# A hybrid attention and RWKV-7 trunk step: prices of the builder's clock, and attention steps ordered a quarter microsecond behind it

## The chip, the cores and the metric

One NeuronCore of one Trainium2 chip. The metric is the device time of one execution in microseconds; of several executions the median counts.

## The reference

One layer of a streaming encoder runs on 512 prompt tokens and on 8 streams of 16 new tokens, 640 tokens in all, with a model width of 1024:

```python
h = rmsnorm(x, norm_g)
proj = h @ w_in                      # [q k v z_a | g_a g_b | r k v lat_w lat_a z_b]
# A: stick-breaking attention, 16 heads of 64, weight
#    sigmoid(z[t,s]) * prod_{s<j<t} (1 - sigmoid(z[t,j])), s < t
y_a = (o_a * silu(z_a)) @ w_o_a
# B: RWKV-7 with a token shift, state S per head
S = S * w_t + (S @ -kk_t) (kk_t * a_t) + v_t k_t ;  o_t = S r_t
y_b = (norm(o_b) * silu(z_b)) @ w_o_b
x = x + (sigmoid(g_a) * y_a + sigmoid(g_b) * y_b) @ w_out
y = rmsnorm(x, final_norm_g)
```

All is in float32. The streams bring 128 past keys and values per head and a state of 64 x 64 per head. The outputs are `y`, the new keys and values, the last projected row and the new states.

## The kernel before, in words

**Work.** The tokens lie along the columns, 640 of them. A projection is a *job*: 128 columns of a weight matrix, split into a high and a low part (`whi`, `wlo`) by ScalarE and VectorE, against `xh` and `xl`, the split input, in two halves of some 320 tokens. Each half is 8 steps of three matmuls (`gemm_range`, L500), so a job has 48 matmuls into the PSUM tiles `ps_g`. There are 73 jobs of the input projection that feed both mixers, then 8 for the gate of B (`cons_gb`), 8 with `w_o_b`, 8 with `w_o_a`, and last `w_out`. The last gate job frees `xh` and `xl` part by part (`xfree`); the stream `reload` (L1542) then fills them with mixer B's output `oB` and, when attention has ended, fills `oAh` and `oAl` with mixer A's output. The jobs with `w_o_b` wait for those parts, those with `w_o_a` for `oAh`.

**RWKV stage.** For each of 8 pairs of heads there are streams `prep`, `prep2`, `samp` and `chain`. `samp` reads the sample states, four transfers into `s0r` (`state_load`, L718: 64 partitions, three dimensions), and transposes them. Its small products use 16, 32 or 64 rows of the array.

**Attention stage.** When RWKV's last pair is done, `open_attn` (L1569) spawns for each pair of heads `aprep` (loads, transposes of keys and values) and `attn` (L1294). `attn` goes through nine items: one for the samples and eight blocks of prompt queries (4, 4, 3, 3, 2, 2, 1, 1 key blocks). For each there is a `score` (two matmuls into `ps_a`; two sigmoids on ScalarE to `kp` and `bt`; a mask on `bt` by POOL; a running product of `kp` and a product into `bt` on VectorE), two items later a `flip` (transposes of `bt` into `ps_b`, copied to `wt`), and then `pv` (products with the values into `ps_c`). In `pv` of the sample item there are 16 products with the past values `Vp`, of 16 columns each, and 4 of 64 columns.

**What sets the order.** The program is written out once, at build time, in one order per engine, and each engine goes through its instructions in that order. The order comes from a clock that the builder keeps: every instruction that is issued goes through `_Eng` (L206), which gives it a duration by operation and shape, and `Clock.note` (L136) moves the engine's time on and notes when each tile will be ready. `Driver.run` (L304) looks at TensorE's time `now` and takes the stream of the highest rank whose awaited tiles are ready by then (`at <= now + 0.02`). If there is none, the main program goes on, and that is the next step of a projection. Only when the main program has to wait as well is the stream taken that will be ready first. Ranks: `chain` 0, `reload` 1, `prep2`, `samp` and `attn` 2, `prep` and `aprep` 3; a lower number goes first. All transfers are issued by SP.

The lines of the choice, with `s[2]` the awaited tiles:

```python
at = self.clk.at(s[2])
if at <= now + 0.02 and (best is None or s[:2] < best[:2]):
    best = s
if soon is None or at < soon[0]:
    soon = (at, s)
```

In the profile every instruction that goes through the builder's wrapper has line L214, so groups are told apart by tiles. A product of two float32 tiles stands in it as two matmuls, one of float32r tiles as one.

Of the kernel before, what the change touches and what calls it, by code (L numbers as in the profile page):

```python
# [162 lines left out]
def _name(ap):  # L163

    if not hasattr(ap, "tensor"):
        return ap
    n = ap.tensor.name
    return f"{n}:{ap.offset % (8 * T) // T}" if n in PARTS else n


def _cols(ap):
    n = 1
    for d in ap.shape[1:]:
        n *= d
    return n
# [30 lines left out]
class _Eng:  # L206
# [3 lines left out]
    def __getattr__(self, op):  # L210
        f = getattr(self.obj, op)

        def call(*a, **k):
            r = f(*a, **k)  # L214
            aps = [x for x in list(a) + list(k.values()) if hasattr(x, "tensor")]
            out = k.get("out", aps[0])
            ins = [x for k, x in enumerate(aps) if x is not out or any(x is y for y in aps[:k])]
            n = _cols(out)
            e = self.eng
            lat = Clock.LAT  # L220
            if e == "pe":
                w = k.get("lhsT")
                m, r = (128, 128) if w is None else (_cols(w), w.shape[0])
                if w is None:
                    d = 0.109
                elif w.dtype == F32R:
                    d = max(0.013 + n / 2400.0, 0.107)
                elif w.dtype == F32:
                    d = max(0.026 + n * 0.00087, 0.082 if m > 32 else 0.041) if m <= 64 else \
                        max(n / 600.0 + 0.005, 0.216)  # L230
                else:
                    d = 0.089
                mode = "full" if r > 64 and m > 64 else (r > 32, r > 64, m > 32, m > 64)
                if mode != self.clk.mode:
                    d += 0.1 if self.clk.mode == "full" else 0.2
                    self.clk.mode = mode
            elif e == "act":
                d = 0.065 + n * 0.00085 + 0.1 * sum(hasattr(k.get(x), "tensor") for x in ("scale", "bias"))
                if out.shape[0] < 64:
                    d = 0.12 + n * 0.0021  # L240
                elif out.shape[0] < 128:
                    d += 0.115
                fn = str(k.get("func"))
                t = "sig" if "Sigmoid" in fn or "Tanh" in fn else "exp" if "Exp" in fn else \
                    "sqrt" if "Sqrt" in fn else None
                if t is not None and t != self.clk.tbl:
                    self.clk.tbl = t
                    d += 1.28
            elif e == "dve":
                d = 0.075 + n * 0.00106  # L250
                if op == "scalar_tensor_tensor":
                    d = 0.13 + n * 0.00112
                elif op == "tensor_scalar":
                    d = 0.1 + n * 0.0011 + 0.03 * sum(hasattr(x, "tensor") and _cols(x) == 1
                                                     for x in list(a) + list(k.values()))
                elif op == "tensor_tensor_scan":
                    d = 0.03 + n * 0.0025
                elif op == "reciprocal":
                    d = 0.05 + n * 0.0064
                elif op == "bn_stats":  # L260
                    d = 0.126
                elif op == "transpose" and len(ins[0].shape) > 2 and ins[0].ap[-1][0] > 1:
                    d = 2.03
                if out.shape[0] < 128 and any(_name(x).startswith("ps_") for x in ins if hasattr(x, "tensor")):
                    d += 0.09
            elif e == "pool":
                d = 0.2 + n * (0.0022 if op == "tensor_tensor" else 0.0012)
                if op == "tensor_copy":
                    d = 0.15 + n * 0.0035
            else:  # L270
                d = 0.47
                run = 2.0 if min(x.shape[-1] for x in aps) < 128 else 1.0
                lat = (n * out.shape[0] * 4 * run / 3.6e5, 0.65, 0.93)
            self.clk.note(e, d, [_name(x) for x in ins], [_name(out)], lat)
            return r
        return call


class Driver:
# [6 lines left out]
        self.streams = []  # L286
        self.n = 0

    def spawn(self, gen, prio):
        self.n += 1  # L290
        self.streams.append([prio, self.n, [], None, gen])

    def _step(self, s):
        try:
# [9 lines left out]
    def run(self, main):  # L304
        gate, done, need = None, False, []
        while not done or self.streams:
            now = self.clk.free["pe"]
            self.each(now)
            best, soon = None, None
            for s in self.streams:  # L310
                if s[3] is not None:
                    if not s[3]():
                        continue
                    s[3], s[2] = None, []
                at = self.clk.at(s[2])
                if at <= now + 0.02 and (best is None or s[:2] < best[:2]):
                    best = s
                if soon is None or at < soon[0]:
                    soon = (at, s)
            if best is not None:  # L320
                self._step(best)
                continue
            if not done and (gate is None or gate()):
                gate = None
                at = self.clk.at(need)
                if at <= now + 0.02 or soon is None or at <= soon[0]:
                    need = []
                    try:
                        y = next(main)
                    except StopIteration:  # L330
                        done = True
                        continue
                    if callable(y):
                        gate = y
                    elif y is not None:
                        need = list(y)
                    continue
            assert soon is not None, "streams wait on each other"
            self._step(soon[1])


def body(tc, ins, outs, dbg=None):
# [4 lines left out]
    drv = Driver(clk)  # L347
    es = ExitStack()

    def pool(name, bufs=1, side="left", **kw):  # L350
        return _Pool(clk, tc.tile_pool(name=name, bufs=bufs, side=side, reuse_waits="tile", **kw),
                     name, bufs)
# [828 lines left out]
    at, ap = {}, {}  # L1181
# [240 lines left out]
    with tc.manual_schedule():  # L1422
# [146 lines left out]
        def open_attn():  # L1569
            if ap:  # L1570
                return
            es3.close()
            es1.close()
            tr_cm.__exit__(None, None, None)
            h["m"] = es.enter_context(pool("m")).tile([128, 8, T], F32, name="m")
            ap["rl"] = es.enter_context(pool("rl"))
            ap["ap2"] = es2.enter_context(pool("ap2", bufs=2))
            ap["ap1"] = es2.enter_context(pool("ap1", bufs=1))
            ap["as2"] = es2.enter_context(pool("as2", bufs=3))
            ap["msk"] = ap["ap1"].tile([128, 640], F32, name="amsk")  # L1580
            dma(out=ap["msk"], in_=ins["consts"][:, NC:NC + 640])
            bft = ap["as2"].tile([128, 256], F32, tag="kp", name="bft", bufs=2)
            dma(out=bft, in_=ins["consts"][:, NC + 640:NC + 896])
            ap["bf"] = ap["ap1"].tile([128, 3, 128], BF16, name="bfc")
            V.tensor_copy(ap["bf"][:, 0, :], ident)
            V.tensor_copy(ap["bf"][:, 1:3].rearrange("p q x -> p (q x)"), bft)
            for p in range(NPAIR):
                drv.spawn(aprep(p), 3)
                drv.spawn(attn(p), 2)

        def open_oa():
            if "mgh" in h:
# [25 lines left out]
        def program():  # L1618
# [7 lines left out]
            for i in range(nbm):  # L1626
                if flags.get(("post", 7)):
                    open_attn()
                yield from gemm_range(i, i + 1)
            yield flag("post", 7)  # L1630
            open_attn()
            drv.spawn(shift_rows(), 3)
            drv.spawn(reload("oB", ap["rl"], 6, "xfree", xh, xl), 1)
# [146 lines left out]
```

## Time and profile before

| | |
|---|---|
| median of 3 runs | 1158.27 us (1156.38 to 1159.37) |
| the profiled execution, its time | 1159.46 us |
| its span, first to last instruction | 1157.7 us |
| TensorE, VectorE, ScalarE, POOL busy | 1107.9, 751.0, 630.9, 392.1 us |
| mean granted clock of TensorE | 0.992 of full speed |
| DMA | 130.70 MB, 113 GB/s in the mean |

Stages by the timeline: start and transposes of the input to some 30 us, RWKV with projections to some 720, projections alone to 738.9, attention with projections to 957.6, then the products with `w_o_b`, `w_o_a` and `w_out`. The time of an execution is a little over its span, as the table shows; a change is judged against the median.

How to read the rows: "PE" is TensorE's matmuls, "PEld" its loads of weights, "DVE" VectorE, "ACT" ScalarE, "SPq" the queue of SP, which issues transfers. An instruction's name is out<-in. A number in square brackets is the time that the engine sat idle before it, with what ended the wait. Matmuls are pipelined, so one that lasts 0.31 us may be followed by the next after 0.15 us; starts, not lengths, tell the pace.

### The profile page before, as it was taken

What the parts mean: (1) busy time and instruction counts of PE and PEld (TensorE: products, weight loads), DVE (VectorE), ACT (ScalarE), POOL (GpSimd) and SP (SyncE); (2) the same over time, 40 slices, a digit from 0 to 9 for tenths busy, and PEclk for the clock granted to TensorE, in tenths of its full rate; (3) what the DMA queues carried; (4) which work ended last, traced back from release to release, by engine and by line L of the source; (5) the groups of instructions that cost most, each with busy time, mean ns of one, the idle gap of its engine ahead of it and who ended that gap; (6) DMA issues with size and microseconds to landing.
All of it is one profiled execution on the core that took longest, in us unless ns stands there. A gap on an engine that the chain in (4) does not pass through costs nothing. (4 is left out here: it accounts for less than half of the span.)

```text
span 1157.7 us, 25429 instructions
## 1 busy us (share of the span) xinstructions
PE 1107.9 (96%) x10050; PEld 1034.6 (89%) x10050; DVE 751.0 (65%) x1517; ACT 630.9 (54%) x1347; POOL 392.1 (34%) x605
## 2 busy tenths in 40 slices
PE   6999999999999999999999999998998998999997
PEld 4989899999999999899898999987887787999997
DVE  6487875855967778777783533577767775535324
ACT  5636466485595775858756465555555551123123
POOL 3030706234161361513615021445445434103302
PEclk9999999999999999999999999999999999999999
DMA  5222222233132142222323244966677525354412
GB/s 194 79 82 73 69 74 67 77 100 110 39 112 73 56 118 61 79 72 57 112 68 90 95 118 135 265 182 180 181 216 202 148 72 161 111 163 141 146 47 91
DMA packets 205294, 130.70 MB, mean 113 GB/s; under 512 B 78332, under 2 KB 184696, under 8 KB 205176
## 3 DMA queue, kind: packets, MB, share of 16 engines
q1 hardware_dynamic: 204888, 129.03, 37.9%
q8 instruction: 79, 1.29, 0.5%
q14 instruction: 39, 0.32, 0.1%
q0 software_dynamic: 288, 0.05, 0.0%
HBM read 97.70 MB, written 31.35 MB: 111 GB/s over the span
## 5 line engine op out<-in xcount | busy, mean ns | idle before, releaser
L214 PE MATMUL ps_g<-xh,whi 128*128 128x320 f32 (+1 forms) x1424 | 468.9, 329 | 1.1 <-ACT xh L214 1.1
L214 PE MATMUL ps_g<-xl,whi 128*128 128x320 f32 (+1 forms) x1424 | 443.0, 311 | 4.6 <-DVE xl L214 4.6
L214 PE MATMUL ps_g<-xh,wlo 128*128 128x320 f32 (+1 forms) x1424 | 442.2, 311 | 1.1 <-DVE wlo L214 1.1
L214 PEld LDWEIGHTS ps_g<-xh,whi 128*128 128x128 f32 x1424 | 270.5, 190 | 8.7 <-issue 3.4
L214 PEld LDWEIGHTS ps_g<-xl,whi 128*128 128x128 f32 x1424 | 270.4, 190 | 8.2 <-DVE xl L214 6.5
L214 PEld LDWEIGHTS ps_g<-xh,wlo 128*128 128x128 f32 x1424 | 269.5, 189 | 2.2 <-DVE wlo L214 2.2
L214 DVE TENSOR_TENSOR wlo<-raw,whi 128x1024 fp32r<-128x1024 f32 x97 | 123.9, 1277 | 71.3 <-ACT whi L214 70.5
L214 ACT ACTIVATE whi<-raw 128x1024 fp32r<-128x1024 f32 x97 | 102.5, 1056 | 82.3 <-PE ps_g L214 55.7
L214 DVE TENSOR_TENSOR_SCAN kp<-kp,amsk 128x256 f32<-128x256 f32 (+3 forms) x80 | 73.7, 930 | 31.6 <-ACT kp L214 31.4
L214 POOL TENSOR_TENSOR bt<-bt,amsk 128x128 f32<-128x128 f32 x64 | 44.7, 702 | 117.0 <-ACT bt L214 98.5
L214 ACT ACTIVATE kp<-ps_a 128x512 f32<-128x512 f32 (+3 forms) x72 | 33.1, 459 | 60.4 <-PE ps_a L214 31.7
L214 ACT ACTIVATE sp<-ps_g 128x320 f32<-128x320 f32 x80 | 35.0, 438 | 52.9 <-PE ps_g L214 42.6
L214 POOL TENSOR_TENSOR itmp<-INV 128x28 f32<-128x28 f32 (+6 forms) x112 | 46.5, 415 | 39.4 <-DVE INV L214 32.0
L214 ACT ACTIVATE RH<-ps_b 128x128 f32<-128x128 f32 (+1 forms) x64 | 19.4, 303 | 69.2 <-PE ps_b L214 69.0
L214 DVE SCALAR_TENSOR_TENSOR X<-ps_b,wc,SW 64x64 f32<-64x64 f32 x96 | 27.0, 282 | 45.7 <-PE ps_b L214 44.4
L214 ACT ACT_TABLE_LOAD x39 | 50.0, 1283 | 10.9 <-DVE BK L214 7.6
L214 POOL TENSOR_TENSOR wl<-wd,wh 128x256 fp32r<-128x256 f32 x8 | 7.2, 905 | 134.0 <-issue 109.1
L214 PE MATMUL ps_b<-cst,bt 128*128 128x128 f32 x192 | 33.8, 279 | 15.8 <-DVE bt L214 14.8
L214 DVE TENSOR_TENSOR bt<-bt,kp 128x511 f32<-128x511 f32 (+4 forms) x72 | 43.6, 605 | 8.2 <-POOL bt L214 0.6
L214 POOL TENSOR_TENSOR INV<-INV,itmp 128x28 f32<-128x28 f32 (+6 forms) x112 | 45.9, 410 | 8.8
L214 POOL TENSOR_TENSOR ux<-X,cst 128x256 f32<-128x256 f32 x32 | 20.3, 653 | 75.6 <-PE ps_b L214 44.7
L214 PE MATMUL ps_g<-olo,mgh 128*128 128x256 f32 x160 | 45.0, 281 | 0.0
(252 smaller groups left out, 2346.2 us busy)
## 6 DMA issues: line engine op xcount, KB each, us to landing
raw<-in_w_in_dram SPq DMA_DIRECT2D x81, 512.0 KB
q<-dr_q SPq DMA_DIRECT2D x32, 160.0 KB
Kr<-in_cache_sb_k_dram SPq DMA_DIRECT2D x16, 256.0 KB
Vp<-in_cache_sb_v_dram SPq DMA_DIRECT2D x16, 256.0 KB
raw<-in_w_o_b_dram SPq DMA_DIRECT2D x8, 512.0 KB
raw<-in_w_o_a_dram SPq DMA_DIRECT2D x8, 512.0 KB
oraw<-in_w_out_dram SPq DMA_DIRECT2D x4, 1024.0 KB
dr_zB<-zm SPq DMA_DIRECT2D x8, 320.0 KB
```

What stands on the lines that cost most here:

```text
L214: r = f(*a, **k)
```

## The change

Three things of the builder change, and nothing of what is computed. The price of float32 matmuls on its clock is changed for products with few rows or columns. A transfer into a target with three or more dimensions and under 128 partitions is priced at 0.62 in place of 0.47 us of issue. And each stream gets a slack, 0 for all but `attn`, 0.25 us there, which is added to the time at which its awaited tiles are ready, where it awaits any.

```diff
--- before.py
+++ after.py
@@ -226,8 +226,8 @@
                 elif w.dtype == F32R:
                     d = max(0.013 + n / 2400.0, 0.107)
                 elif w.dtype == F32:
-                    d = max(0.026 + n * 0.00087, 0.082 if m > 32 else 0.041) if m <= 64 else \
-                        max(n / 600.0 + 0.005, 0.216)
+                    d = (0.155 if r <= 64 else max(n / 600.0 + 0.005, 0.216)) if m > 64 else \
+                        0.005 + n * 0.0011 if r <= 32 else 0.026 + n * 0.00087
                 else:
                     d = 0.089
                 mode = "full" if r > 64 and m > 64 else (r > 32, r > 64, m > 32, m > 64)
@@ -268,7 +268,7 @@
                 if op == "tensor_copy":
                     d = 0.15 + n * 0.0035
             else:
-                d = 0.47
+                d = 0.62 if len(out.shape) > 2 and out.shape[0] < 128 else 0.47
                 run = 2.0 if min(x.shape[-1] for x in aps) < 128 else 1.0
                 lat = (n * out.shape[0] * 4 * run / 3.6e5, 0.65, 0.93)
             self.clk.note(e, d, [_name(x) for x in ins], [_name(out)], lat)
@@ -276,6 +276,9 @@
         return call
 
 
+SLACK2 = 0.25
+
+
 class Driver:
 
 
@@ -286,9 +289,10 @@
         self.streams = []
         self.n = 0
 
-    def spawn(self, gen, prio):
+    def spawn(self, gen, prio, slack=0.0):
+
         self.n += 1
-        self.streams.append([prio, self.n, [], None, gen])
+        self.streams.append([prio, self.n, [], None, gen, slack])
 
     def _step(self, s):
         try:
@@ -313,6 +317,8 @@
                         continue
                     s[3], s[2] = None, []
                 at = self.clk.at(s[2])
+                if s[2]:
+                    at += s[5]
                 if at <= now + 0.02 and (best is None or s[:2] < best[:2]):
                     best = s
                 if soon is None or at < soon[0]:
@@ -1586,7 +1592,7 @@
             V.tensor_copy(ap["bf"][:, 1:3].rearrange("p q x -> p (q x)"), bft)
             for p in range(NPAIR):
                 drv.spawn(aprep(p), 3)
-                drv.spawn(attn(p), 2)
+                drv.spawn(attn(p), 2, SLACK2)
 
         def open_oa():
             if "mgh" in h:
```

## Rows read from the trace of the kernel before

**Rows 1.** The page's engine part: busy us (share of the span) xinstructions.
```profile
PE 1107.9 (96%) x10050; PEld 1034.6 (89%) x10050; DVE 751.0 (65%) x1517; ACT 630.9 (54%) x1347; POOL 392.1 (34%) x605
```

**Rows 2.** Table of stretches: stretch, length, each engine's busy us (instructions), clock, DMA share, GB/s.
```profile
30.00:690.00 660.00, 646.83 (x6400) 609.78 (x6400) 461.51 (x1044) 418.18 (x888) 225.72 (x405) 1.00 0.28 82
738.90:957.60 218.70, 202.64 (x1861) 175.73 (x1860) 161.56 (x221) 122.85 (x293) 97.78 (x121) 0.99 0.62 172
957.60:990.50 32.90, 29.02 (x170) 27.49 (x171) 22.95 (x22) 5.77 (x9) 18.34 (x16) 0.90 0.58 178
```

**Rows 3.** Waits, TensorE, stretch 700 to 957: us in total, times, longest us.
```profile
PE ps_b L214 <- DVE bt L214: 14.8, 20, 2.0
```

**Rows 4.** Timeline, TensorE, fourth pair: start us, us, instruction, [idle before <- what ended it].
```profile
830.18 0.34 PE L214 MATMUL ps_c<-wt,vtok 128*64 128x64 f32 x4
...
831.46 0.44 PE L214 MATMUL ps_a<-ks,qh 128*128 128x384 f32 x1
...
832.48 0.28 PE L214 MATMUL ps_a<-ks,ql 128*128 128x256 f32 x1
833.39 0.52 PE L214 MATMUL ps_b<-cst,bt 128*128 128x128 f32 x3 [0.64 <-DVE bt L214]
833.67 0.39 PE L214 MATMUL ps_g<-xh,whi 128*128 128x320 f32 x1
833.90 0.31 PE L214 MATMUL ps_g<-xl,whi 128*128 128x320 f32 x1
```

**Rows 5.** Timeline, VectorE, in front of the same flip.
```profile
831.07 1.36 DVE L214 TENSOR_TENSOR_SCAN kp<-kp,amsk 128x384 f32<-128x384 f32 x1
832.53 0.72 DVE L214 TENSOR_TENSOR bt<-bt,kp 128x383 f32<-128x383 f32 x1
```

**Rows 6.** The chain that ended last, behind attention: start us, us, what.
```profile
957.60 11.21 PE ps_g L214 x75
```

**Rows 7.** Timeline, refills behind attention: on POOL, and the last two on VectorE.
```profile
968.89 9.35 POOL L214 TENSOR_SCALAR xh<-rl 128x640 fp32r<-128x640 f32 x8 [14.12 <-PE ps_g L214]
978.96 3.21 POOL L214 TENSOR_SCALAR oAh<-rl 128x640 fp32r<-128x640 f32 x3 [0.73 <-DMA rl<-dr_oA]
...
989.21 2.08 DVE L214 TENSOR_TENSOR oAl<-rl,oAh 128x640 fp32r<-128x640 f32 x2
```

**Rows 8.** Timeline, TensorE, the first product with w_o_b.
```profile
977.71 0.42 PE L214 MATMUL ps_g<-xl,whi 128*128 128x320 f32 x1 [2.21 <-DVE xl L214]
...
978.97 0.64 PE L214 MATMUL ps_g<-xl,whi 128*128 128x320 f32 x1 [0.55 <-DVE xl L214]
979.40 0.47 PE L214 MATMUL ps_g<-xh,wlo 128*128 128x320 f32 x1
979.67 0.47 PE L214 MATMUL ps_g<-xh,whi 128*128 128x320 f32 x1
```

**Rows 9.** Table of stretches of 5 us; the granted clock stands behind the five engines.
```profile
920.00:925.00 5.00, 4.48 (x31) 4.01 (x32) 4.75 (x8) 1.75 (x5) 3.08 (x4) 0.66 0.92 251
...
975.00:980.00 5.00, 2.24 (x10) 1.72 (x10) 5.00 (x5) 0.00 (x0) 4.27 (x4) 0.83 0.93 311
980.00:985.00 5.00, 4.98 (x19) 4.58 (x18) 4.00 (x5) 0.00 (x0) 4.69 (x6) 0.50 0.79 224
```

**Rows 10.** The view of tile s0r: its issues on SP's queue, ns min/median/max.
```profile
L214 SPq DMA_DIRECT2D s0r<-in_state_wkv_dram x32: 596/621/698, 111.0 to 624.2; - x32
```

**Rows 11.** Waits, TensorE, stretch 30 to 690.
```profile
PE ps_a L214 <- DMA s0r<-in_state_wkv_dram: 4.8, 5, 1.4
```

**Rows 12.** Groups by shape, stretch 100 to 690: xcount | busy us, mean ns.
```profile
L214 PE MATMUL ps_a<-H,BK 64*128 64x128 f32 x280 | 21.8, 288 | 1.5 <-POOL H L214 1.5
...
L214 PE MATMUL ps_a<-STG,AB 16*32 16x16 f32 x512 | 5.9, 184 | 0.0
```

**Rows 13.** The view of tile bt, stretch 745 to 957: ns min/median/max.
```profile
L214 POOL TENSOR_TENSOR bt<-bt,amsk x63: 455/621/1395, 744.7 to 954.3; 128x128 f32<-128x128 f32 x63
```

**Rows 14.** Table of stretches, instructions on the projections' PSUM tile ps_g alone.
```profile
935.70:957.60 21.90, 10.53 (x59) 8.75 (x58) 0.00 (x0) 1.22 (x3) 1.00 0.28 72
```

## Prediction

> **What bounds the kernel now.** The page's engine part comes first: TensorE is busy for 96% of the span [rows 1], so the total is TensorE's work plus its idle time, and only idle time, a lowered clock or a dearer order can change it: the diff adds and removes no instruction and no wait; it changes the order. The table of stretches then says where the idle time lies [rows 2]: 660.00 - 646.83 = 13.2 us in the RWKV stage, 218.70 - 202.64 = 16.1 us in the attention stage, 3.9 us in the stretch behind it. In attention VectorE is busy for 161.56 of 218.70 us, so it does not bound the stretch by itself.
>
> The view of waits for the attention stage names what TensorE's matmuls wait for: 14.8 us in 20 waits (mean 0.74, longest 2.0) for `bt` from VectorE [rows 3], that is for the weights that `flip` transposes. The timeline shows one: the last score of 256 columns starts at 832.48, nothing stands behind it but the flip, and the flip comes 0.64 us late, at 833.39; projection matmuls that were ready all along follow at 833.67 [rows 4]. VectorE is then in its product of `bt`, from 832.53 for 0.72 us [rows 5]. TensorE takes its instructions in the order in which the builder wrote them, and the builder thought that `bt` was ready.
>
> The chain of waits shows what is behind: after the last attention step at 957.60, 75 projection matmuls run in 11.21 us [rows 6], 0.1495 us each, so one step of a projection (three matmuls) is 0.448 us. This is the end of the last gate job, which frees `xh`. Then `xh` is refilled from 968.89 by copies on POOL [rows 7], and TensorE waits for `xl`: three gaps of 0.55 (one stands) and one of 2.21, 3.9 us in all [rows 8]. The granted clock falls with it: 0.83 and 0.50 of full speed in two stretches of 5 us [rows 9], the lower of its two levels (1.2 of 2.4 GHz) for (0.17 x 5 + 0.50 x 5)/0.5 = 6.7 us. There matmuls follow each other by 979.67 - 979.40 = 0.27 us in place of 0.1495 [rows 8], so 6.7 x (1 - 0.1495/0.27) = 3.0 us are lost. Tail: 6.9 us.
>
> **The change part by part.** Only the builder's order changes, by three edits.
>
> *A. Slack and the 16-column products.* A step of `attn` that waits for a tile counts as ready 0.25 us later. And the 16 products with `Vp` of each pair (64 columns of weights, 128 rows) cost the clock 0.026 + 16 x 0.00087 = 0.040 us in place of 0.082. Their block, 20 products, runs from 830.18 to 831.46 [rows 4], 1.28 us; the clock had 20 x 0.082 = 1.64 and now has 4 x 0.082 + 16 x 0.040 = 0.97, with 0.2 for the change of tile shape on either, so 1.84 and 1.17. So 0.67 us per pair come free on the builder's clock just ahead of the flip of rows 4. With 0.25 of slack that is 0.92 us, two projection steps (0.90 us) where now none stands. Each of the 8 pairs has this place, since all run the same items; at the mean wait of 0.74 it goes: 8 x 0.74 = 5.9 us. The other 12 waits gain what 0.25 us lets in, 12 x 0.25 = 3.0. Sum 8.9; I take **8.5**, because some waits are shorter than the step put before them. Bounds: all 16.1 us, and nothing. A loss is excluded as long as projections are left, since TensorE works in the time that it would have waited. They are: 75 + 8 jobs of 48 matmuls = 459, 153 steps, are left behind attention.
>
> *B. Issue of transfers with three dimensions and under 128 partitions: 0.62 in place of 0.47.* The loads `s0r` are such (64 partitions); their issue takes 0.621 median [rows 10], so the clock was 0.15 short, four times in a row. It now sees the last of the four land 0.6 us later and puts projections ahead of the transposes that read them. TensorE waits for `s0r` 4.8 us in 5 waits [rows 11], 0.96 each; 5 x 0.6 = 3.0. I take **2.5**, bounds 0 and 4.8. The queue of SP itself issues the same transfers, each as long as before; its order shifts by a place here and there, which costs nothing while the transfers in question are issued many microseconds ahead (in attention the raw weights, `kT`, `q`, `Kr`, `Vp`).
>
> *C. The tail.* A and B put more projections into attention: two steps per pair at the place of rows 4 and about two more at the other waits, 8 x 4 = 32 steps. 25 steps stand behind attention now. So the last gate job would end some 7 steps before attention does, and the refill of `xh` would run beside the last pair. It is not free there: eight copies on POOL (968.89 to 978.25 [rows 7], 1.17 us each) and eight subtractions on VectorE come between the masks and scans, and the projections of that time wait for them. I take half of 6.9: **3.5**; bounds 0 and 6.9. If the cover is gone, the tail stays at 6.9 and C is nothing.
>
> *D. The clock in attention.* 0.66 of full speed in 920 to 925 [rows 9], 3.4 us at the lower level behind a wait of about 2 us, costs 3.4 x 0.45 = 1.5 us. With two steps put into that wait: **1.0**; bounds 0 and 1.5.
>
> *E. The other matmul prices.* In the RWKV stage the products of `H` and `BK` (r = 64) fall from 0.218 to 0.155 on the clock; the trace, in which each of these products stands as two matmuls, has 21.8 us for 280, 0.156 a product [rows 12]. Those of 16 columns with r = 16 or 32 fall from 0.041 to 0.023; the trace has 5.9 us for 512, 0.023 a product [rows 12]. Per pair 20 x 0.063 + 80 x 0.018 + 32 x 0.014 + 16 x 0.028 = 3.6 us come free, eight projection steps, 64 in all. They lengthen the RWKV stage and shorten what is left for later; on TensorE's total that is nothing by itself. What it does to the waits is not to be seen in the trace; the nearest row bounds it, 13.2 us of idle time in that stage, 8.4 without `s0r` [rows 2, 11]. A step put off can wake a new wait as well as end one: **0**, with 8 us to either side as the extreme and 5 as what I carry.
>
> *F. Seams.* Behind a flip the first projection matmul takes 833.90 - 833.67 = 0.23 us in place of 0.15 [rows 4]. Some 20 new places where projections come between two attention steps: 20 x 0.08 = 1.6. I take **1.5** as a loss; bounds 0 and 4 (50 places).
>
> Sum: 8.5 + 2.5 + 3.5 + 1.0 - 1.5 = 14.0 us. The profiled execution took 1159.46 us (span 1157.7), 1.2 above the median of the runs, 1158.27. So 1145.5 against itself and 1144.3 against the median: **1145**.
>
> **The rivals.** *1. The flip only moves, and the wait with it.* VectorE still holds a scan and a product when the flip comes (1.36 and 0.72 us in rows 5); if its backlog sets the pace also on the builder's clock, slack shifts the phase once per pair and the score behind the flip comes later too. For it: in that stretch VectorE goes from one to the next without a gap. Against it: over the stage it is 74% busy. Then A, C, D and F are nothing and B stays: 1158.3 - 2.5 = **1156**. That the slack acts on nothing, since most steps are ready long before TensorE reaches them, gives the same time. The masks on POOL take 0.455 us at least, 0.621 in the median and 1.395 at most [rows 13], for one shape. The Trainium skill (GPSIMD Engine Reference, section Specifications) says that POOL shares its SBUF interfaces with VectorE and contends with VectorE instructions that have two SBUF inputs, as the products of `bt` are; by that rule 63 x (0.621 - 0.455) = 10.5 us of lateness would belong to the machine and not to the order, and A would be 16.1 - 10.5 = 5.6 us at most, so the sum would be 11 us. The trace agrees with the spread and does not show its cause.
>
> *2. Slower: the projections run out.* Attention then ends when the products with `w_o_b` are used up, and the refill of `oAh` and `oAl` stands bare: from 978.96 to 991.29, 12.3 us now covered [rows 7], plus the last pair without projections (59 matmuls [rows 14], 8.8 us idle), plus the lower clock as in rows 9 (3.0): 24.1. Against it stand A to F with the tail gone wholly: 8.5 + 2.5 + 6.9 + 1.0 - 1.5 = 17.4. So +6.7: **1165**. It decides when more than 153 - 12.3/0.448 = 126 steps are used up; I count 32 + 64 = 96, and the 64 only if the RWKV stage takes all of them.
>
> *3. Everything goes.* Slack adds steps at most waits, also those that were short: A 15, B 4.8, C 6.9, D 1.5, F -2: 26 us, **1132**. For it: the steps that are put in stay in, so a pair that runs late on VectorE is helped by each of them.
>
> **How the numbers follow.** About 0.3%, 3.5 us, is what a measurement of this kernel can tell from no change: below 1154.8 is faster, above 1161.7 slower. Forecast 0.49, rival 1 0.20, rival 2 0.09, rival 3 0.12, a shifted order in the RWKV stage that takes back more than the 5 us of E 0.10. Faster: 0.49 + 0.12 + 0.07 of rival 1 + 0.03 of the last = 0.71. Same: 0.13 + 0.04 = 0.17. Slower: 0.09 + 0.03 = 0.12. The forecast with its terms at half and with E against it is 1145 + 7 + 5 = 1157; rival 1 ends at 1156, with E's small side at 1160. Below, 1133 takes in most of rival 3. Range 1133 to 1160; left out are rival 2 and the ends, near 0.17.
>
> **What would show it.** Right: in the changed profile the wait of `flip` for `bt` falls from 14.8 us to 4 to 8; TensorE's idle time in attention from 16.1 to under 9 though the stage itself grows longer; the wait for `s0r` from 4.8 to about 2; fewer than 75 projection matmuls between the last attention step and the refill of `xh`, gaps for `xl` under 2 us and no stretch of 0.50 there; the last pair holds more than its 59 projection matmuls [rows 14]. Wrong: 14 us of waits for `bt` as before (rival 1); a gap before the first product with `w_o_a` (rival 2); idle time in the RWKV stage above 18 us (E).

## The result and the profile after

The changed kernel takes 1168.89 us (median of 5 runs, 1166.57 to 1174.46), the kernel before beside it 1159.37 us (5 runs, 1156.38 to 1161.74): a ratio of 1.0087 [1.0063, 1.011]. It is slower by 0.9%, where 1145 was forecast. The profiled execution took 1167.85 us, its span 1166.1 us.

The page's engine part of the changed kernel, which answers to [rows 1]:

```profile
PE 1112.2 (95%) x10050; PEld 1038.1 (89%) x10050; DVE 742.6 (64%) x1517; ACT 628.0 (54%) x1347; POOL 398.0 (34%) x605
```

The span grew by 8.4 us: TensorE is busy for 4.3 us more and idle for 1166.1 - 1112.2 = 53.9 in place of 1157.7 - 1107.9 = 49.8 us. The mean granted clock fell from 0.992 to 0.983 over the same 10,050 matmuls; how much of the 4.3 us is the clock's is not shown, since a run below has 5.1 us less busy time than the kernel before at the same 0.992.

The table of stretches says where. Columns: stretch, length, busy us (instructions) of TensorE's matmuls, its weight loads, VectorE, ScalarE and POOL, granted clock, DMA share, GB/s. The changed kernel, answering to [rows 2]:

```profile
30.00:690.00 660.00, 645.43 (x6355) 609.82 (x6355) 451.81 (x995) 403.24 (x849) 225.33 (x397) 1.00 0.29 83
690.00:775.50 85.50, 85.38 (x637) 83.43 (x635) 34.58 (x107) 47.22 (x103) 18.46 (x18) 1.00 0.49 140
775.50:1030.30 254.80, 234.62 (x2062) 208.91 (x2061) 176.55 (x247) 124.13 (x291) 105.60 (x129) 0.96 0.58 161
1030.30:1036.10 5.80, 5.80 (x42) 5.80 (x40) 2.41 (x3) 0.08 (x1) 3.77 (x4) 1.00 0.63 182
1036.10:1166.10 130.00, 118.38 (x865) 115.18 (x864) 57.83 (x126) 36.38 (x74) 34.58 (x41) 0.97 0.38 127
```

The same view of the kernel before, behind its attention stage:

```profile
957.60:1036.00 78.40, 74.52 (x480) 72.99 (x481) 38.13 (x42) 12.13 (x15) 18.34 (x16) 0.96 0.45 139
1036.00:1157.70 121.70, 113.99 (x866) 113.27 (x864) 50.81 (x118) 36.38 (x74) 30.57 (x37) 0.99 0.35 115
```

The first product with `oAh`, that is with mixer A's output, comes at 1036.1 us in the one and at 1036.0 in the other. Up to there nothing was won, and all of the 8.3 us lies behind it (130.0 against 121.7). Attention starts 36.6 us later, since more projections run in front of it, and lasts 254.8 in place of 218.7 us; only 5.8 us of projections are left behind it, in place of 78.4.

In the view of waits, TensorE from 775 to 1062 (us in total, times, longest), the forecast wait is gone, and others stand in its place; [rows 3] had 14.8 us for `bt`:

```profile
PE ps_g L214 <- DVE xl L214: 9.7, 3, 7.7
PE ps_g L214 <- DVE wlo L214: 6.7, 2, 6.1
PE ps_g L214 <- DVE oAl L214: 2.1, 3, 1.2
...
PE ps_g L214 <- POOL oAh L214: 1.3, 1, 1.3
...
PE ps_b L214 <- DVE bt L214: 0.4, 1, 0.4
```

Waits for `s0r`, from 30 to 775 us, fell from the 4.8 us of [rows 11] to 0.3:

```profile
PE ps_a L214 <- DMA s0r<-in_state_wkv_dram: 0.3, 1, 0.3
```

And ScalarE has a wait in attention that it had once in the kernel before. The changed kernel:

```profile
ACT sg L214 <- DMA dr_oA<-sg: 26.4, 5, 6.1
```

The kernel before:

```profile
ACT sg L214 <- DMA dr_oA<-sg: 4.5, 1, 4.5
```

**How that wait comes about.** `sg` holds sigmoid and gate of a pair and then its output; it has one buffer. The last product of a pair writes the output into it, SP stores it (`dr_oA<-sg`), and only when the store has been read out may ScalarE write the next pair's sigmoid. The builder issues a store when the clock says that the tile has been ready for 3 us (`MARGIN`, L43), when the buffer is wanted again, or when the stored tensor is to be read. The timelines of the changed kernel, first the last product of the first pair on VectorE and the first score of the second pair on TensorE (start us, us, instruction, [idle before <- what ended it]):

```profile
803.93 0.69 DVE L214 TENSOR_TENSOR sg<-ps_c,sg 128x512 f32<-128x512 f32 x1 [2.71 <-PE ps_c L214]
...
803.81 0.43 PE L214 MATMUL ps_a<-KT,qbd 128*32 128x128 f32 x8
```

SP's queue, then ScalarE, POOL, VectorE and TensorE, as the delay goes on:

```profile
805.84 0.36 SPq L214 DMA_DIRECT2D kT<-dr_k  x1
806.30 2.42 SPq L214 DMA_DIRECT2D q<-dr_q  x4
...
811.87 1.33 SPq L214 DMA_DIRECT2D Vp<-in_cache_sb_v_dram  x2
813.29 2.54 SPq L214 DMA_DIRECT2D dr_oA<-sg  x1
...
818.60 0.74 ACT L214 ACTIVATE sg<-sz 128x640 f32<-128x640 f32 x1 [5.33 <-DMA dr_oA<-sg]
...
819.41 1.58 POOL L214 TENSOR_TENSOR sg<-sg,sz 128x640 f32<-128x640 f32 x1 [6.05 <-ACT sg L214]
...
821.02 0.29 DVE L214 TENSOR_TENSOR sg<-ps_c,sg 128x128 f32<-128x128 f32 x1 [6.18 <-POOL sg L214]
...
826.02 1.22 DVE L214 TENSOR_TENSOR wlo<-raw,whi 128x1024 fp32r<-128x1024 f32 x1
...
827.30 0.63 PE L214 MATMUL ps_g<-xh,wlo 128*128 128x320 f32 x1 [6.08 <-DVE wlo L214]
```

The product ends at 804.62, behind the first score of the next pair. By then the loads of a later pair have been put into SP's order, so the store is issued at 813.29, 8.7 us late. ScalarE stands for 5.33 us, POOL and VectorE behind it for 6, and TensorE runs out of split weights for 6.08 us. In the kernel before, the last product of the first pair ended at 765.55 and its store was issued at 765.57; the next pair's first score came at 766.7:

```profile
764.86 0.69 DVE L214 TENSOR_TENSOR sg<-ps_c,sg 128x512 f32<-128x512 f32 x1 [0.55 <-PE ps_c L214]
...
765.57 0.32 SPq L214 DMA_DIRECT2D dr_oA<-sg  x1
```

In the changed kernel the product ends 0.8 to 0.9 us behind the next pair's first score in 4 of 7 pairs and 0.3 ahead of it in one; these five stores are issued 8.1 to 9.9 us after the product, the others within 0.1. In the kernel before it ends ahead in all seven, once by only 0.3 us (848.4 against 848.7): there the store goes out at 858.5, 10.1 us after the product, and there its one wait of 4.5 us lies. The issue of a late store also takes longer on SP: 1.41 to 2.54 us in the changed kernel, where one issued on time takes 0.33 or 0.34.

**The refill of `xh`.** The projections in front of and in attention rose to 3465 and 797 matmuls on `ps_g` (from 3225 and 596), so the last gate job ends in the middle of attention, and the refill of [rows 7] begins at 911.3 us, 119 us before attention ends, among scans, masks and the late `sg`. The timelines of POOL, VectorE and TensorE:

```profile
913.65 3.60 POOL L214 TENSOR_SCALAR xh<-rl 128x640 fp32r<-128x640 f32 x3
917.37 1.96 POOL L214 TENSOR_TENSOR sg<-sg,sz 128x640 f32<-128x640 f32 x1
...
922.67 4.33 POOL L214 TENSOR_SCALAR xh<-rl 128x640 fp32r<-128x640 f32 x4
...
925.08 5.53 DVE L214 TENSOR_TENSOR xl<-rl,xh 128x640 fp32r<-128x640 f32 x6
...
926.47 0.64 PE L214 MATMUL ps_g<-xl,whi 128*128 128x320 f32 x1 [7.75 <-DVE xl L214]
```

The gap for `xl` was 2.21 us before [rows 8]; here it is 7.75, in a stage in which steps of attention are queued behind that matmul. A row of the table of stretches shows the clock that goes with it, 0.50 (the lower level) for 13.7 us, in which TensorE works for 5.96 us and is idle for the 7.75:

```profile
918.50:932.20 13.70, 5.96 (x33) 5.08 (x32) 12.27 (x16) 4.01 (x12) 9.79 (x12) 0.50 0.54 161
```

**The refill of `oAh` stands bare.** TensorE and POOL behind attention:

```profile
1037.54 0.41 PE L214 MATMUL ps_g<-oAl,whi 128*128 128x320 f32 x1 [1.17 <-DVE oAl L214]
...
1040.87 4.11 POOL L214 TENSOR_SCALAR oAh<-rl 128x640 fp32r<-128x640 f32 x4 [6.59 <-DMA rl<-dr_oA]
...
1041.64 0.64 PE L214 MATMUL ps_g<-oAh,whi 128*128 128x320 f32 x1 [1.33 <-POOL oAh L214]
```

Of the 8.3 us behind the first product with `oAh`, 3.9 are idle time (11.6 us against 7.7). The rest is busy time; the clock is at 0.64 and 0.68 in the two stretches of 5 us from 1040 to 1050, which makes 6.8 us at the lower level.

### The profile page after: what moved, and what is told of

It reads as the page before. It is cut to its first block, busy times and chain, and to the rows that moved or that the text cites. A ratio compares the mean times of both kernels' runs of the same rounds, so it can differ in the third digit from the quotient of the medians.

```text
span 1166.1 us, 25424 instructions
## 1 busy us (share of the span) xinstructions
PE 1112.2 (95%) x10050; PEld 1038.1 (89%) x10050; DVE 742.6 (64%) x1517; ACT 628.0 (54%) x1347; POOL 398.0 (34%) x605
## 5 line engine op out<-in xcount | busy, mean ns | idle before, releaser
L214 POOL TENSOR_TENSOR itmp<-INV 128x28 f32<-128x28 f32 (+6 forms) x112 | 49.7, 443 | 61.8 <-DVE INV L214 54.1
L214 ACT ACTIVATE kp<-ps_a 128x512 f32<-128x512 f32 (+3 forms) x72 | 33.0, 458 | 66.7 <-PE ps_a L214 53.9
L214 POOL TENSOR_TENSOR INV<-INV,itmp 128x28 f32<-128x28 f32 (+6 forms) x112 | 48.4, 433 | 8.8
L214 POOL TENSOR_TENSOR H<-R,E 64x512 f32<-64x512 f32 (+1 forms) x32 | 32.9, 1046 | 38.8 <-PE ps_c L214 38.2
L214 ACT ACTIVATE wt<-ps_b 128x512 f32<-128x512 f32 (+3 forms) x72 | 32.9, 465 | 23.8 <-PE ps_b L214 23.6
```

## The experiments

Each ratio is to the kernel before on the same chip (median 1159.5 to 1160.3 us there), with its 95% interval; it is not exactly the quotient of the two medians. The first four runs take the change apart and free the buffer in two ways. Two theories stand against each other: that the late store costs the time, or that the projections moved in front of attention do ("supply").

**Slack alone.** The changed kernel with the old prices:

```diff
-                    d = (0.155 if r <= 64 else max(n / 600.0 + 0.005, 0.216)) if m > 64 else \
-                        0.005 + n * 0.0011 if r <= 32 else 0.026 + n * 0.00087
+                    d = max(0.026 + n * 0.00087, 0.082 if m > 32 else 0.041) if m <= 64 else \
+                        max(n / 600.0 + 0.005, 0.216)
...
-                d = 0.62 if len(out.shape) > 2 and out.shape[0] < 128 else 0.47
+                d = 0.47
```

> The slack alone, with the old prices. Late-store theory (the slack puts the last product of a pair behind the first score of the next, so its store goes out late, and ScalarE stands some 5 us in the next pair for the one buffer of sg): 3 or more waits of ScalarE for the store dr_oA, as the 5 in the changed kernel, pairs of over 33 us, and 1163 to 1172 us. Supply theory (the cheaper products move projections into the RWKV stage, so that the refill of xh falls into the middle of attention): attention starts within 5 us of 739 as before, the refill stays near its end, and the waits for bt are gone, 1145 to 1155 us.

Measured: 1162.33 us, 1.0018 [1.0007, 1.003]. The waits of ScalarE and TensorE in its attention stage:

```profile
ACT sg L214 <- DMA dr_oA<-sg: 24.9, 5, 6.5
...
PE ps_g L214 <- DVE wlo L214: 8.3, 2, 7.6
...
PE ps_b L214 <- DVE bt L214: 6.4, 9, 1.6
```

The slack alone brings the five waits for the store, and waits for `bt` fall by 8.4 us. The stage takes 249.8 us, nearly as long as in the changed kernel (254.8), though it begins at 739.8, as before. The time is just under the 1163 to 1172 us of the late-store theory. That it is no slower than 0.2% fits the projections that are left: 50 us of them cover the refill of `oAh`, and the rest behind the first product with it is 120.6 us, not 130.0.

**Prices alone.** The changed kernel with `SLACK2 = 0.0`.

> The new prices alone, slack 0. Late-store theory: at most 2 waits of ScalarE for the store dr_oA, waits for bt partly back (5 to 15 us), wait for s0r under 1 us, 1148 to 1158 us. Supply theory: attention starts at 770 or later, the refill of xh comes well inside attention with gaps for xl of 8 us or more, 1163 to 1170 us.

Measured: 1152.75 us, 0.9932 [0.9914, 0.9949]: faster. Waits for `bt` are 5.9 us in 9, for the store 10.0 us in 2 (4.6 and 5.3), and 20.7 us of projections cover the refill of `oAh` (first product with it at 1026.8, attention's end at 1006.1). So the prices by themselves take 8.9 us from the waits for `bt`. Attention starts at 777.5 us, as the supply theory has it, and the loss that this theory expects does not come: the longest wait for `xl` is 2.7 us.

**A second buffer for `sg`.** The changed kernel with:

```diff
-                sg = ap["ap1"].tile([128, T], F32, tag="oAf", name="sg")
+                sg = ap["ap1"].tile([128, T], F32, tag="oAf", name="sg", bufs=2)
```

> The changed kernel with two buffers for sg, so that ScalarE need not wait for the store of the pair before. Late-store theory: no wait of ScalarE for dr_oA (26.4 us in 5 in the changed kernel), the gap of 6.1 us for wlo gone, pairs near 28 us, 1148 to 1158 us. Supply theory: the waits of ScalarE go, the gaps for xl and for oAl stay (10 and 3 us with their lower clock), 1162 us or more.

Measured: 1146.04 us (4 runs, 1144.25 to 1151.72), 0.9884 [0.9861, 0.9907]. ScalarE no longer waits for a store. TensorE's waits in attention (us in total, times, longest):

```profile
PE ps_b L214 <- DVE bt L214: 4.7, 5, 1.1
PE ps_g L214 <- DVE xl L214: 1.9, 1, 1.9
```

Its table of stretches, from the start of attention:

```profile
775.90:999.90 224.00, 214.88 (x1948) 190.01 (x1947) 177.53 (x240) 122.77 (x288) 109.44 (x129) 0.98 0.65 176
999.90:1022.40 22.50, 22.50 (x155) 22.50 (x154) 14.46 (x18) 3.18 (x3) 7.25 (x8) 1.00 0.68 217
1022.40:1145.20 122.80, 114.24 (x866) 113.26 (x864) 50.72 (x118) 36.40 (x74) 30.62 (x37) 0.98 0.34 116
```

Idle time in attention is 9.1 us (20.2 without the buffer, 16.1 before), the stage ends 30 us earlier than in the changed kernel, 22.5 us of projections cover the refill, and the rest is 122.8 us. Attention starts at 775.9, as in the changed kernel, so the moved projections alone do not make the loss. One word in an allocation turns +0.9% into -1.2%, so the single buffer carries the loss. How much of the difference is its own is less sure, because the order moves as well: the refill of `xh` falls better here (a wait of 1.9 us in place of 9.7) than in most orders below. This version beats both kernels.

**The store issued at once.** The changed kernel, with one buffer, and the store not left to the margin:

```diff
         to_dram(("oA", p), tmp)
+        fetch("oA", p)
```

> The changed kernel, where the store dr_oA is put into SP's order right behind the last product of its pair, ahead of the loads of a later pair. Late-store theory: ScalarE's waits for dr_oA under 8 us in all, 1148 to 1160 us. Supply theory: as with two buffers, 1162 us or more.

Measured: 1149.43 us, 0.9893 [0.9873, 0.9914], the intervals of this and of the second buffer overlap. Seven of the eight stores are issued within 0.1 us of the product; one comes 5.0 us late (product 934.4, store 939.4), and there alone ScalarE waits:

```profile
ACT sg L214 <- DMA dr_oA<-sg: 9.9, 1, 9.9
```

In four of seven pairs the product still ends 0.8 us behind the next pair's first score, and ScalarE doesn't wait there. So it is the place of the store in SP's order, not a product 0.8 us late, that costs. TensorE's wait for `ktok`, 1.1 us in the changed kernel, is 3.6 here; whether the earlier place of the store brings that is not shown.

**The same wait in the kernel before.** Its output stores are not issued by the margin, only when the buffer is wanted; nothing else changes:

```diff
-    drv.each = lambda now: flush(lambda e: clk.ready.get(e[0], 0.0) + MARGIN <= now)
+    drv.each = lambda now: flush(lambda e: clk.ready.get(e[0], 0.0) + MARGIN <= now and (e[3] or "x")[0] != "oA")
```

> The kernel before, with neither slack nor new prices, but with the store dr_oA held back until the next pair takes the buffer of sg. Late-store theory: ScalarE waits for the store in 6 or 7 pairs (1 in the kernel before), about 5 us each, pairs of 31 us and more, 1165 to 1178 us. If the late store is only a sign of something else (attention steps that come late for another reason): at most 1162 us.

Measured: 1186.44 us, 1.023 [1.0197, 1.0263]. The waits in its attention stage:

```profile
ACT sg L214 <- DMA dr_oA<-sg: 47.8, 6, 12.5
...
PE ps_g L214 <- DVE wlo L214: 16.2, 2, 8.4
PE ps_g L214 <- POOL xh L214: 7.3, 1, 7.3
PE ps_b L214 <- DVE bt L214: 6.5, 8, 1.6
```

Late stores alone make the picture of the changed kernel: ScalarE stands, weights come late, attention grows to 281.9 us. It is more of it: the six stores go out 10 to 19 us after the product, where the five of the changed kernel took 8.1 to 9.9, and the time lies above the 1165 to 1178 us expected. Waits for `bt` fall too, without slack and without prices, which fits a VectorE that gets through its backlog while ScalarE stands. So the fall to 0.4 us in the changed kernel is not all gain: with two buffers it is to 4.7.

**Two buffers in the kernel before, with slack, with prices.** Three kernels: the kernel before, the slack alone and the prices alone, each with `bufs=2`.

> The kernel before with two buffers for sg. Late-store theory: only the one wait of 4.5 us goes, 1156 to 1160 us. If the second buffer is itself the gain of the run with two buffers: 1144 to 1150 us.

> Slack alone with two buffers for sg. Late-store theory with my term A as forecast (8.5 us of waits for bt go, less seams): 1147 to 1154 us, no wait of ScalarE for dr_oA. If the slack costs by itself (longer pairs, seams): 1157 us or more.

> The new prices alone with two buffers for sg. Late-store theory: the two waits left in the run with the prices alone (9.9 us in all) go, 1146 to 1152 us. If those waits were covered by projections: 1152 to 1154 us, as with one buffer.

Measured (ratio to the kernel before; waits for `bt` and `xl` in attention and the refill, in us):

| | one buffer | two buffers | `bt`, `xl` with two |
|---|---|---|---|
| kernel before | 1 | 0.9997 [0.998, 1.0014] | 14.5, 3.5 |
| slack alone | 1.0018 [1.0007, 1.003] | 0.9966 [0.9952, 0.998] | 8.9, 3.3 |
| prices alone | 0.9932 [0.9914, 0.9949] | 0.9972 [0.995, 0.9994] | 4.4, 5.7 |
| both | 1.0087 [1.0063, 1.011] | 0.9884 [0.9861, 0.9907] | 4.7, 1.9 |

With two buffers the medians are 1160.25, 1155.72 and 1155.78 us. The first is what the late-store theory expected, within 0.3 us; the slack alone lies between its two expectations, and the prices alone above both of theirs. The buffer is worth nothing where only one store is late (the kernel before), 0.5% with the slack, and 2.0% with both. With prices alone it costs 0.4%, though the two waits for the store go. The refill of `xh` falls on another place there: TensorE waits 4.92 us for `xl`, and the clock is at the lower level for 10.2 us from 933.9 on.

```profile
934.52 0.63 PE L214 MATMUL ps_g<-xl,whi 128*128 128x320 f32 x1 [4.92 <-DVE xl L214]
```

With one buffer that wait is 2.7 us at most, and the mean clock in attention is 1.00. So a refill beside attention can be dear with no wait for a store in it.

**The two prices apart.** The kernel before with the price of transfers alone, and with the prices of matmuls alone (the lines of the diff of the change).

> The kernel before with the new price of transfers alone. My term B: the waits of TensorE for s0r fall from 4.8 to about 2 us, attention starts within 3 us of 739, 1155 to 1159 us. If the later start of attention comes from this price: a start at 760 or later.

> The kernel before with the new prices of matmuls alone. My terms A (price part) and E: attention starts at 770 to 785 (64 steps, 29 us, and more), the waits for bt fall from 14.8 to 5 to 9 us, the waits for s0r stay near 5, 1150 to 1157 us. If E's idle time of the RWKV stage moves: above 18 us there, 1158 us or more.

The transfer price alone: 1164.43 us, 1.0036 [1.0022, 1.005], above what was expected; attention starts at 752.2, between the two starts that were named. The matmul prices alone: 1165.44 us, 1.0055 [1.0037, 1.0072]. Attention starts at 774.0 and the waits for `bt` fall to 6.5 us, as expected, but the time is that of the second case, idle time in the RWKV stage. The page's engine part of the kernel with the transfer price:

```profile
PE 1112.2 (96%) x10050; PEld 1038.7 (89%) x10050; DVE 748.4 (64%) x1517; ACT 629.5 (54%) x1347; POOL 396.2 (34%) x605
```

Its idle time is that of the kernel before (1161.6 - 1112.2 = 49.4 us against 49.8), and the waits for `s0r` are gone from the list as B said; what is longer is busy time, by 4.3 us, at a mean clock of 0.985 against 0.992. The kernel with the matmul prices, first its RWKV stage in the table of stretches, then two waits of TensorE there:

```profile
30.00:690.00 660.00, 637.51 (x6256) 601.19 (x6256) 465.08 (x1021) 403.01 (x847) 225.35 (x397) 0.99 0.28 80
```

```profile
PE ps_a L214 <- DVE BK L214: 4.8, 3, 1.9
PE ps_g L214 <- DVE wlo L214: 3.5, 3, 1.6
```

TensorE is idle there for 22.5 us in place of 13.2: with projections moved into this stage, new waits wake, the loss to which E gave 8 us at the extreme. In the changed kernel, where both prices act, it is 14.6. Why the transfer price takes that back, and why its own order shows a lower clock, stays open. ScalarE waits for no store in either of these two kernels, so their loss is of another kind.

**Other slacks.** Two buffers, with `SLACK2 = 0.5` and `0.12`.

> All edits, two buffers for sg, and a slack of 0.5 in place of 0.25. If the gain is in filling waits for bt: those were 4.7 us with 0.25, so at most 4 us more, 1142 to 1147 us, attention some 8 us longer. If a longer attention uses up the projections (cover behind attention 22 us with 0.25, and about 15 needed): below 15 us, idle time before the products with w_o_a, 1148 us or more.

> All edits, two buffers for sg, slack 0.12. If the gain grows with the slack: between 1155.8 (0) and 1146 (0.25), 1148 to 1153 us, waits for bt 5 to 9 us. If the order jumps rather than slides: outside of that range on either side.

Measured: 1153.28 us, 0.9936 [0.9912, 0.996], and 1156.17 us, 0.9974 [0.995, 0.9997]. Waits for `bt` are 2.2 and 4.7 us, for `xl` 8.1 and 6.3. Both lie above the ranges for a gain by slack; the cover at 0.5 is 23.7 us, so the projections didn't run out either. The waits for `bt` are least at the largest slack, as A says, and the total doesn't follow. What stands out at 0, 0.12 and 0.5 is the refill of `xh` in attention, with a longest wait for `xl` of 4.9, 4.5 and 5.6 us, each with 10.2 us at the lower clock around it; at 0.25 it is 1.9, with 6.8 us at the lower clock. The order jumps, and 0.25 is a lucky place in it rather than a best slack.

## Why the prediction was wrong

**A and B, right in what they removed.** Waits for `bt` fell from 14.8 to 0.4 us (to 4.7 with two buffers, 10.1 less), those for `s0r` from 4.8 to 0.3, more than the 8.5 and 2.5 that were taken. Rival 1, that the flip only moves, is out: with the slack alone and two buffers, where ScalarE waits for no store, the waits for `bt` fell to 8.9 us. The Trainium skill (GPSIMD Engine Reference, Specifications) has POOL and VectorE contend for SBUF, by which A, in the estimate of the prediction, could be at most 5.6 us. The masks are no faster than in [rows 13] (median 0.660 us), and with two buffers 10.1 us of the waits went all the same, so at least that much of the lateness was one of the order.

**The step that failed** is in A: "A loss is excluded as long as projections are left". It counted TensorE alone. The slack puts steps of `attn` later, and the last step frees `sg` by way of a store. The same blind spot stands in B, that SP issues each transfer "as long as before" and that its order "shifts by a place here and there, which costs nothing": five stores shifted by 8 to 10 us behind loads, and their issue took 1.41 to 2.54 us in place of 0.3. What the runs show in its place is a wait of ScalarE for the one buffer, 26.4 us in five pairs. Slack alone and late stores alone each bring it, and the second buffer gives 1168.89 - 1146.04 = 22.9 us back. Not all of that is the wait. An estimate: against the two neighbouring slacks with two buffers (1156.17 and 1153.28 us) it is 13 to 16 us, and the other 7 to 10 are the lucky place of the refill at 0.25; no run has those slacks with one buffer.

**C had the wrong sign.** It counted the 32 steps of A and B, not the 64 that E moves in front of attention, and so had the refill beside the last pair; it came 119 us before the end. The refill beside attention cost 9.7 us for `xl` where 3.9 stood before and 3.5 were to be gained, with 13.7 us at the lower clock. It is dear with a late `sg` among POOL's copies (7.75 us) and without one (4.92 us with the prices and two buffers); with both and two buffers it costs 1.9.

**D** came out the other way, with a mean clock of 0.96 in attention and 0.99 before; the refill of `xh` alone has 13.7 us at the lower level. **E** was 0 in the changed kernel within 1.4 us (14.6 against 13.2 idle), but with the matmul prices alone the idle time there is 9.3 us more. **F** was not tested alone.

**Rival 2 had the mechanism and 0.09.** Its count was too small: 96 steps by my sum, 126 as the point from which it decides. In the trace (240 + 201)/3 = 147 steps were used up before attention ended, partly by slack and prices, partly because the longer stage drew them in while ScalarE stood. The refill of `oAh` then stood bare and cost 8.3 us, where 12.3 and 3.0 of clock were priced (and 8.8 for a last pair without projections, which didn't come). The clock came as priced (6.8 us at the lower level), the idle time was 3.9 us: four of the eight parts could be copied in time. The 12.3 itself was read from rows that end too early. The last group on VectorE in [rows 7] is three subtractions, to 992.02, not two to 991.29. The 1165 of this rival is nearest to 1168.89, though what lengthened the stage was not in it.

With the one wait taken away the changed order takes 1146.04 us, near the forecast of 1145; the sum of 14.0 stood for the work of the order and lacked the buffer. That nearness is partly luck, as slacks of 0.12 and 0.5 show (1156.17 and 1153.28 us). And it isn't confirmed term by term: with two buffers idle time fell by 49.8 - (1145.2 - 1102.8) = 7.4 us and busy time by 5.1, and I did not find what the latter belongs to.

## What to carry to other kernels

Before steps of a stream are delayed, look at what its last step sets free: a single buffer that leaves by a store is in the path, and the store's place in the queue moves with it. Cover (work that fills waits) is a stock to be counted over all stages, with what a longer stage draws, because the refill behind it stands bare when it is used up. Where a builder picks greedily by a clock, prices and slack make the order jump: gains of two edits do not add (with two buffers 0.9966 for the slack, 0.9972 for the prices, together 0.9884), and each order is to be measured.

## What was unexpected of the hardware

- From the issue of the store of 128 x 640 float32 at 813.29 to ScalarE's start at 818.60 it takes 5.3 us. The Trainium skill (DMA: Bandwidth & Descriptors, Latency and other measured facts) names HBM access, 0.2 us in the mean and 2 under load, as the main part of a transfer's fixed cost. The 5.3 us here are with the loads of a pair just ahead in the queue; what each part took, no run here shows.
- The clock falls at other places with the same order. The slack alone and the second buffer alone act only in attention; yet from 80 to 85 us and from 135 to 140 the granted clock is 0.66 and 1.00 in the kernel before, 0.70 and 0.66 with slack alone, 1.00 and 1.00 with the second buffer alone. One short fall in one profile is no finding about an order.
